# Batch norm with ReLU: the second half of x loaded as 14 and 2 rows per partition, its result stored in two transfers, and rows 4 to 15 of the first half in one

## The chip, the cores and the metric

One core of a Trainium2 chip. The metric is the device time of one execution in microseconds (us). Each ratio is to the kernel before in the same rounds; comparisons of traces cross chips.

## The reference

```python
# x: (32, 128, 32, 32) float32, 16.78 MB; the parameters: 128 values each
normalized = (x - running_mean[None, :, None, None]) / np.sqrt(running_var[None, :, None, None] + eps)
scaled = normalized * gamma[None, :, None, None] + beta[None, :, None, None]
return np.maximum(scaled, 0).astype(np.float32)
```

Each (image, channel) pair is a row of 1024 values, 4 KB. A row gets one scale and one bias, so ScalarE does it in one activation. The rest is moving 16.78 MB in and 16.78 MB out.

## The kernel before

x is seen as 2 halves of 128 partitions of 16 rows. A partition's 16 rows lie one after another in memory, 64 KB, so a transfer of n rows moves one run of 4n KB per partition. Loads are issued by SyncE, stores by ScalarE's queue.

```python
J = 16
TILES = ((0, 0, 2), (0, 2, 4), (0, 4, 8), (0, 8, 16), (1, 0, 16))   # half, first row, row after the last
LOAD_CUTS = {(1, 8)}      # a tile's load is cut here
STORE_CUTS = {(0, 1)}     # a store goes out before this row
HALVES = {(0, 0), (0, 1)} # rows done in two activations
...
    for t, a, b in TILES:
        xt = data.tile([P, b - a, HW], F32, name=f"x{t}_{a}")
        cuts = [a] + [j for j in range(a + 1, b) if (t, j) in LOAD_CUTS] + [b]
        for c, d in zip(cuts, cuts[1:]):
            nc.sync.dma_start(out=xt[:, c - a : d - a, :], in_=xr[t, :, c:d, :])
...
        for t, a, b, xt in tiles:                    # in this order on ScalarE
            first = a
            for j in range(a, b):
                # ... one ReLU activation (two for rows 0 and 1), in place
                if j + 1 == b or (t, j + 1) in STORE_CUTS:
                    nc.scalar.dma_start(
                        out=outr[t, :, first : j + 1, :], in_=xt[:, first - a : j + 1 - a, :]
                    )
                    first = j + 1
```

So before, the loads are 2, 2, 4, 8 rows of the first half and 8, 8 of the second; the stores are 1, 1, 2, 4, 8 rows of the first half and 16 of the second. The whole of x stays in on-chip memory; no buffer is used twice.

## Time and profile before

| | kernel before |
|---|---|
| median time, range of 3 runs | 83.81 us, 83.73 to 83.94 |
| span in the profile | 82.0 us |
| ScalarE busy | 39.1 us, 48% |
| first to last big DMA packet | 1.80 to 80.80 us, DMA busy share 1.00 |
| bytes | 16.78 MB read, 16.78 MB written |

The lines behind this are in the prediction. They are read like this: a busy share of 1.00 over all but 3 us means that the time is bytes over rate plus two ends; a wait of any other engine costs only if it leaves the DMA queues empty. One view belongs here too, because the change acts on it: the order of time of the second half on ScalarE (start, duration, engine, line, what, how often, and the wait ahead of it).

```profile
34.85 9.16 ACT L102 ACTIVATE x<-x,bias_t,scale_t 128x1024 f32<-128x1024 f32 x8 [1.78 <-DMA x<-in_x_dram]
46.87 9.16 ACT L102 ACTIVATE x<-x,bias_t,scale_t 128x1024 f32<-128x1024 f32 x8 [2.86 <-DMA x<-in_x_dram]
56.05 0.34 ACTq L110 DMA_DIRECT2D out_dram<-x  x1
```

Eight rows as soon as their load has landed, eight more after the next load, then one store of all sixteen.

### The profile page before, as it was taken

Reading aid. Unit: us, or ns where it says so; the run is one execution under the profiler, and the core shown is the slowest. Engines: PE = TensorE matmul, PEld = TensorE weight load, DVE = VectorE, ACT = ScalarE, POOL = GpSimd, SP = SyncE. Lnnn points to the kernel's source line nnn. Section 1 sums busy time; section 2 is a strip of 40 time slices with the busy share of each in tenths; the row PEclk is TensorE's granted clock in tenths of the full one; section 3 lists DMA queues with packets and bytes.
Section 4 is the critical chain, followed back from the end, with each engine's and each line's share of the span. In section 5 each row is a group of like instructions: output and inputs, shape, how many; then the busy total and the mean of one; then the engine's idle time right before and its main releaser. Section 6 shows DMA issues by size and latency. Waiting matters only on the chain.

```text
span 82.0 us, 120 instructions
## 1 busy us (share of the span) xinstructions
PE 0.7 (1%) x2; PEld 0.5 (1%) x2; DVE 0.8 (1%) x5; ACT 39.1 (48%) x36; POOL 0.8 (1%) x6
## 2 busy tenths in 40 slices
PE   0002000000000000000000000000000000000000
PEld 0002000000000000000000000000000000000000
DVE  0000300000000000000000000000000000000000
ACT  0600477799239999199994199993000000000000
POOL 3000000000000000000000000000000000000000
DMA  2899997979899989999799799998992999996590
GB/s 48 336 424 456 416 544 336 524 322 526 338 434 430 506 358 506 390 434 444 320 460 500 316 424 448 512 432 368 480 736 128 416 512 512 512 512 288 224 512 0
DMA packets 1792, 33.56 MB, mean 409 GB/s; under 512 B 256, under 2 KB 256, under 8 KB 512
## 3 DMA queue, kind: packets, MB, share of 16 engines
q1 hardware_dynamic: 864, 16.78, 48.7%
q10 hardware_dynamic: 928, 16.78, 47.6%
HBM read 16.78 MB, written 16.78 MB: 409 GB/s over the span
## 4 chain that ended last, share of the span: by engine, by line
DMA 56%; ACT 10%; issue 2%; SPq 0%
DMA x<-in_x_dram 56%; ACT x L102 10%; SPq L56 0%
## 5 line engine op out<-in xcount | busy, mean ns | idle before, releaser
L102 ACT ACTIVATE x<-x,bias_t,scale_t 128x1024 f32<-128x1024 f32 (+1 forms) x34 | 37.5, 1177 | 9.9 <-DMA x<-in_x_dram 7.6
L86 ACT ACT_TABLE_LOAD x1 | 1.3, 1283 | 2.6 <-issue 2.6
L86 ACT ACTIVATE std_t<-cols,eps_t 128x16 f32<-128x16 f32 x1 | 0.3, 273 | 4.5 <-PE cols L78 4.5
L78 PE MATMUL cols<-raw,rep 8*128 8x64 f32 x2 | 0.7, 429 | 7.6 <-DMA raw<-in_beta_dram 7.6
L78 PEld LDWEIGHTS cols<-raw,rep 8*128 8x128 f32 x2 | 0.5, 306 | 7.6 <-issue 7.6
L68 POOL TENSOR_SCALAR_AFFINE_SELECT rep<-rep 8x128 f32<-8x128 f32 x1 | 0.4, 392 | 0.1
L88 DVE RECIPROCAL rstd_t<-std_t 128x16 f32<-128x16 f32 x1 | 0.3, 254 | 7.7 <-ACT std_t L86 7.7
L67 POOL MEMSET rep<- 8x128 f32 x1 | 0.2, 194 | 0.3 <-POOLq L130 0.3
L90 DVE TENSOR_TENSOR scale_t<-cols,rstd_t 128x16 f32<-128x16 f32 x1 | 0.2, 175 | 0.1
L92 DVE TENSOR_TENSOR ms_t<-cols,scale_t 128x16 f32<-128x16 f32 x1 | 0.2, 175 | 0.0
L94 DVE TENSOR_TENSOR bias_t<-cols,ms_t 128x16 f32<-128x16 f32 x1 | 0.2, 174 | 0.0
L130 POOL MEMSET const-bfloat16-1.0<- 128x1 bf16 x1 | 0.1, 106 | 0.0
L130 POOL MEMSET const-uint8-127<- 128x1 uint8 x1 | 0.1, 106 | 0.0
L130 POOL MEMSET const-float32-0.0<- 128x1 f32 x1 | 0.1, 103 | 0.3 <-issue 0.3
L130 POOL MEMSET const-float32-1.0<- 128x1 f32 x1 | 0.1, 103 | 0.0
L65 DVE MEMSET eps_t<- 128x1 f32 x1 | 0.1, 59 | 0.9 <-PEq L130 0.9
## 6 DMA issues: line engine op xcount, KB each, us to landing
x<-in_x_dram SPq DMA_DIRECT2D x3, 4096.0 KB, 38.7
out_dram<-x ACTq DMA_DIRECT2D x1, 4096.0 KB, 28.7
x<-in_x_dram SPq DMA_DIRECT2D x2, 1024.0 KB, 5.8
x<-in_x_dram SPq DMA_DIRECT2D x1, 2048.0 KB, 11.3
out_dram<-x ACTq DMA_DIRECT2D x1, 2048.0 KB
out_dram<-x ACTq DMA_DIRECT2D x2, 512.0 KB, 19.6
out_dram<-x ACTq DMA_DIRECT2D x1, 1024.0 KB
raw<-in_running_var_dram ACTq DMA_DIRECT2D x1, 0.5 KB
```

What stands on the lines that cost most here:

```text
L65: nc.vector.memset(eps_t, float(eps))
L67: nc.gpsimd.memset(rep, 1.0)
L68: nc.gpsimd.affine_select(out=rep, in_=rep, compare_op=mybir.AluOpType.is_equal, fill=0.0, base=0, pattern=[[0, P // Q], [-1, Q]], channel ...
L78: nc.tensor.matmul(cols.rearrange("p k j -> p (k j)"), rep.rearrange("q r s -> q (r s)"), raw.rearrange("q k j -> q (k j)"), start=True, s ...
L86: nc.scalar.activation(out=std_t, in_=cols[:, 0, :], func=ACTF.Sqrt, bias=eps_t[:, 0:1], scale=1.0)
L88: nc.vector.reciprocal(out=rstd_t, in_=std_t)
L90: nc.vector.tensor_mul(out=scale_t, in0=cols[:, 1, :], in1=rstd_t)
L92: nc.vector.tensor_mul(out=ms_t, in0=cols[:, 2, :], in1=scale_t)
L94: nc.vector.tensor_sub(out=bias_t, in0=cols[:, 3, :], in1=ms_t)
L102: nc.scalar.activation(out=xt[:, j - a, w : w + step], in_=xt[:, j - a, w : w + step], func=ACTF.Relu, bias=bias_t[:, j : j + 1], scale=sc ...
L130: nc = _bacc.Bacc("TRN2", target_bir_lowering=False, num_devices=1)
```

## The change

Its apparent intent: give the load queue a long transfer and a short last one, and let half of the second half's result go out earlier, in place of one 8.39 MB store at the end.

```diff
-TILES = ((0, 0, 2), (0, 2, 4), (0, 4, 8), (0, 8, 16), (1, 0, 16))
+TILES = ((0, 0, 2), (0, 2, 4), (0, 4, 16), (1, 0, 16))
 
-LOAD_CUTS = {(1, 8)}
-STORE_CUTS = {(0, 1)}
+LOAD_CUTS = {(0, 8), (1, 14)}
+STORE_CUTS = {(0, 1), (1, 8)}
```

Loads after: 2, 2, 4, 8 and 14, 2. Stores after: 1, 1, 2, 12 and 8, 8.

## The prediction

> **What bounds the kernel now.** I read the page's slices first, then the DMA queues, then busy time by stage, and only then the chain of work that ended last. The kernel reads 16.78 MB and writes 16.78 MB, so the first question is whether the 16 DMA engines ever stand still. The page:
>
> ```profile
> span 82.0 us, 120 instructions
> PE 0.7 (1%) x2; PEld 0.5 (1%) x2; DVE 0.8 (1%) x5; ACT 39.1 (48%) x36; POOL 0.8 (1%) x6
> ...
> DMA  2899997979899989999799799998992999996590
> GB/s 48 336 424 456 416 544 336 524 322 526 338 434 430 506 358 506 390 434 444 320 460 500 316 424 448 512 432 368 480 736 128 416 512 512 512 512 288 224 512 0
> ...
> q1 hardware_dynamic: 864, 16.78, 48.7%
> q10 hardware_dynamic: 928, 16.78, 47.6%
> HBM read 16.78 MB, written 16.78 MB: 409 GB/s over the span
> ```
>
> ScalarE, the busiest compute engine, works 48% of the span. The two queues (q1 loads, q10 stores and the small parameters) take 48.7% + 47.6% = 96.3% of the 16 engines' time over the whole span. The DMA row seems to show holes (a 2 in the 31st slice, a 6 and a 5 near the end), with 736 GB/s just before one and 128 in it. I take these for an artefact: a slice is 2.05 us, and the packets of the last store, 64 KB each, take 2.418 us, so if a packet is booked where it starts, some slices get two rounds and some almost none. To check, I asked for longer stretches, cut where the trace's packet records change character: the first 8 KB packet starts at 1.80 us, the first store packet at 14.60, the last load packet ends at 46.17, the last store packet at 80.80.
>
> ```profile
> 1.80:14.60 12.80, 0.66 (x2) 0.50 (x2) 0.78 (x4) 5.64 (x7) 0.00 (x0) 1.00 1.03 420
> 14.60:46.20 31.60, 0.00 (x0) 0.00 (x0) 0.00 (x0) 24.26 (x22) 0.00 (x0) 1.00 1.00 422
> 46.20:80.80 34.60, 0.00 (x0) 0.00 (x0) 0.00 (x0) 9.16 (x8) 0.00 (x0) 1.00 0.99 429
> ...
> 0.00:1.80 1.80, 0.00 (x0) 0.00 (x0) 0.06 (x1) 0.00 (x0) 0.80 (x6) 1.00 0.00 0
> 1.80:80.80 79.00, 0.66 (x2) 0.50 (x2) 0.78 (x4) 39.06 (x36) 0.00 (x0) 1.00 1.00 425
> 80.80:82.00 1.20, 0.00 (x0) 0.00 (x0) 0.00 (x0) 0.00 (x0) 0.00 (x0) 1.00 0.00 0
> ```
>
> The second number from the end of each line is the DMA engines' busy share: 1.00 over 79.0 us. There are no holes. The span is 1.80 us before the first packet, 79.0 us of saturated DMA, 1.20 us after the last packet. The measured 83.81 us is about 1.8 us more than the span.
>
> Last, the chain, which would mislead if read first:
>
> ```profile
> 8.12 38.72 DMA x<-in_x_dram
> 46.84 0.03 issue
> 46.87 0.04 ACT x L102
> 46.91 1.10 issue
> 48.01 8.01 ACT x L102 x7
> ```
>
> It says: last load, eight activations, last store. But the last store, issued at 56.05 us, has its first packet only at 60.98: its queue was still busy with the store before it. The 8.39 MB of that store alone would be done by about 56.4 + 8.39/0.433 = 75.8 us; the end is 80.8. So the chain has some 4.9 us of slack here, and the bytes set the end.
>
> **What the Trainium skill says.** "DMA: Bandwidth & Descriptors", section Where 436 GB/s comes from, gives a ceiling of 435 GB/s for the 16 engines' ports. The trace agrees: 420 to 429 by stage as the lines count it, and 434 when I spread the packets of the store-only stage evenly over their durations. The same page, section Queues, rings and completion order, says that an engine takes turns between the queue rows that have work, a packet at a time. The trace agrees if one run of bytes per partition counts as the packet: between 14.60 and 35.67 us sixteen 4 KB store packets per engine went by, 1.32 us each, against 1.213 + 0.159 = 1.372 us for one 32 KB load packet plus one 4 KB store packet. "ScalarE: Activation LUTs", section What ACT_TABLE_LOAD costs, gives 186 ns + 0.833 ns per element plus about 93 ns for each per-partition operand: 186 + 853 + 186 = 1225 ns for 1024 elements with two. The trace has 1227 ns for the 30 rows of that shape.
>
> **The change, part by part.** Loads stay six, stores stay six; no byte is added; the activations stay 30 full rows and 4 half rows. The build of the changed kernel confirms it: the same instructions stand on PE, VectorE and GpSimd, and ScalarE and the load queue have other sizes only. The order of semaphore waits is alike too: activation rows still wait for their own load, not for the whole tile.
>
> *DMA work.* Packet times in the trace, by size: 4 KB 159 ns, 8 KB 309, 16 KB 611, 32 KB 1213, 64 KB 2418. That is a line: (2418 - 1213)/32768 = 0.0368 ns per byte plus about 8 ns per packet. From it, estimates for the new sizes: 56 KB 2117 ns, 48 KB 1816 ns. Each engine moves 8 partitions, so it has 8 packets per transfer, 96 in all, before and after. Before, per engine: loads 16 x 0.309 + 8 x 0.611 + 24 x 1.213, stores 16 x 0.159 + 8 x (0.309 + 0.611 + 1.213 + 2.418) = 38.94 + 38.95 = 77.9 us. The remaining 79.0 - 77.9 = 1.1 us is packets that took longer than these medians, about 0.95 us (0.47 at the start, 0.48 between 12 and 48 us, where reads and writes mix), and the engines' uneven start and end. After: loads 24 x 0.309 + 8 x (0.611 + 1.213 + 2.117) = 38.94, stores 16 x 0.159 + 8 x (0.309 + 1.816) + 16 x 1.213 = 38.95; sum 77.9 us. Change: 0.0 us.
>
> *Does any engine starve?* I walked one engine's queues by turns. Until the load of rows 8 to 15 lands nothing differs: ScalarE starts on them at 23.9 us, ends at 33.07, and the store of rows 4 to 15 is issued about 33.1, where the store of rows 8 to 15 was. By about 22.6 us six 4 KB store packets are through. Then eight turns of 56 KB load + 4 KB store: 8 x (2.117 + 0.159) = 18.2, to 40.8 us; the 14 rows land about 42 (in the before trace the landing of rows 8 to 15 came 1.2 us after the same reckoning). Then eight turns with the 8 KB loads, against two 4 KB and six 8 KB stores: 2 x 0.468 + 6 x 0.618 = 4.6, to 45.4 us, landing about 46.5. Loads thus end within 1 us of where they ended. At that point the store queue holds two 8 KB packets and eight 48 KB packets per engine: 0.6 + 14.5 = 15.1 us, enough until about 60.6.
>
> *ScalarE.* It starts the second half at about 42 instead of 34.85 us, 7 us later, but no longer pauses in the middle. Eight rows take 9.16 us, so the first store of the second half is issued about 51.2, needed at 60.6: 9 us in hand. The other eight end at about 60.4 (rows 14 and 15 are in by 46.5), the last store is issued then and needed at 60.6 + 8 x 1.213 = 70.3: 10 us in hand. Then 9.7 us more: 80.0, plus the engines' spread and the slow packets, 80.8 as before. So ScalarE ending some 4 us later than its 56.0 costs nothing, and splitting the last store gains nothing.
>
> Sum: 1.8 + 79.0 + 1.2 = 82.0 us of span, 83.8 us measured.
>
> **The rivals.**
> 1. *The last store is the tail, and halving it shortens the end.* For it: the chain. Against it: DMA share 0.99 to 1.00 to the end. If the chain did bind, ScalarE's end at 60.4 plus 4.19 MB at 0.433 would give about 70 us for the last packet, so 73 us measured. I see no way for 33.5 MB to move in that time.
> 2. *The later ScalarE starves the stores.* It would need the 48 KB store or the first store of the second half to come more than 9 us later than worked out, for instance if its activations waited for the whole tile and the second half's first store went out at 55 to 56 us: still before 60.6. If both second-half stores were held until the very end, ScalarE's 60.4 plus about 3 us of issue to first packet, the hole would be about 3 us: 86.8 us.
> 3. *The mix of reads and writes moves at another rate.* The mixed stage lost 0.48 us to slow packets. Larger load packets leave fewer changes between read and write per megabyte before 41 us and more of them after. That can give back or cost up to that amount: 83.3 to 84.3.
> 4. *A 56 KB or 48 KB run is not moved as one packet.* 64 KB runs are one packet each in the trace, so I expect it. If the 56 KB loads were cut into 4 KB packets, 1664 more packets at 8 ns over 16 engines would be 0.8 us, and taking turns would favour the stores: 84.6 us.
>
> **Range and chances.** Everything that I can size comes to zero within rival 3; the three runs before span 83.73 to 83.94. I predict 83.8 us, 83.3 to 84.3 in 8 of 10 cases. Faster by 2% needs 82.1 us, below what 79 us of saturated DMA plus the two ends and the 1.8 us outside the span allow even without a single slow packet (83.81 - 0.95 = 82.9): 0.01. Slower by 2% is 85.5, which only a starved stage gives (rival 2): 0.02. Within 2%: 0.97.
>
> **What would show it right or wrong.** In the profile of the changed kernel: DMA share near 1.00 from about 1.8 to 80.8 us; 96 packets per engine again, with 128 packets of 56 KB at about 2.12 us and 128 of 48 KB at about 1.82; ScalarE's second half from about 42 to 60.4 us with one wait before it; the last load landing about 46.5; the last store issued about 60.4 and its first packet near 70. It would be wrong if a stretch after 46 us showed a DMA share clearly under 1, if the new sizes appeared as many small packets, or if the packet times of known sizes grew.

## The result, and the profile after

| | before | after |
|---|---|---|
| median of 6 runs each | 83.77 us | 84.18 us |
| range | 83.6 to 83.94 | 84.01 to 84.31 |
| span of the profiled run | 82.0 us | 82.4 us |
| first to last big packet | 1.80 to 80.80 us | 1.81 to 81.19 us |

The ratio is 1.0047, with a 95% interval of 1.0030 to 1.0064. Executions over 1.5% slower than the fastest of the same kernel are left out of the means. Ratios here are the mean time of one kernel's fast runs over that of the other's of the same rounds, so not quite the ratio of the medians. The prediction (83.8 us, 83.3 to 84.3, within 2%) holds; the change is some 0.4 us slower, which is small but clear of the noise. The span belongs to one profiled run; before, that run took 83.68 us and not the median 83.81, so the time lies 1.7 us above the span in both kernels, not the 1.8 of the prediction.

From the page of the changed kernel:

```profile
span 82.4 us, 120 instructions
...
DMA  2899997979799999999489988888996998899690
GB/s 48 318 434 466 414 533 334 549 302 557 302 509 454 469 477 477 477 450 336 169 330 430 712 382 382 382 382 382 573 430 302 477 509 382 382 509 461 302 509 0
...
q1 hardware_dynamic: 864, 16.78, 48.9%
q10 hardware_dynamic: 928, 16.78, 47.4%
```

The packet counts, 864 and 928, are those of before: 96 data packets per engine, as counted in the prediction. The queues' shares sum to 96.3%, again as before. By stage, cut at the first and last big packet (after the name of the stretch its length, the busy time of PE, its weight loads, VectorE, ScalarE and GpSimd, the clock, the DMA share and GB/s):

```profile
0.00:1.81 1.81, 0.00 (x0) 0.00 (x0) 0.06 (x1) 0.00 (x0) 0.79 (x6) 1.00 0.00 0
1.81:81.19 79.38, 0.66 (x2) 0.50 (x2) 0.77 (x4) 39.06 (x36) 0.00 (x0) 1.00 1.00 423
81.19:82.40 1.21, 0.00 (x0) 0.00 (x0) 0.00 (x0) 0.00 (x0) 0.00 (x0) 1.00 0.00 0
```

The two ends are unchanged (1.81 and 1.21 us). The saturated part is 79.38 us instead of 79.00, still at a share of 1.00: the engines do not wait more, they take longer for the same packets. And ScalarE in order of time:

```profile
42.52 9.16 ACT L102 ACTIVATE x<-x,bias_t,scale_t 128x1024 f32<-128x1024 f32 x8 [9.49 <-DMA x<-in_x_dram]
51.70 0.34 ACTq L110 DMA_DIRECT2D out_dram<-x  x1
52.09 9.16 ACT L102 ACTIVATE x<-x,bias_t,scale_t 128x1024 f32<-128x1024 f32 x8 [0.42 <-ACT x L102]
61.27 0.34 ACTq L110 DMA_DIRECT2D out_dram<-x  x1
```

ScalarE waits 9.49 us for the 14 rows, starts the second half 7.7 us later than before and issues the last store 5.2 us later. None of this reaches the end: the first store of the second half goes out at 51.70 us, and the store ahead of it keeps its queue busy until 61.4 to 61.8.

Where are the 0.4 us? In the packet records of the traces, the time of one 56 KB load packet has a median of 2116 ns (the estimate was 2117), but a mean of 2182. All the excess is in one round: each of the 16 engines moves eight such packets, and the last one, begun between 38.7 and 39.4 us, took 2641 ns on average, 25% longer. The other seven of each engine took 2116. (The records carry no engine number; the starts fall into eight bands of 16, and each band is taken for one round.) ScalarE stood idle from 33.4 to 42.52 us, so it is not what slowed that round. From here on I call "slow-packet time" what an engine's load packets begun between 26 and 48 us take beyond the usual time of their size (the medians of before and 912, 1815 and 2116 ns for 24, 48 and 56 KB), averaged over the 16 engines: 0.19 us before, 0.64 us after.

### The profile page after: what moved, and what is told of

It reads as the page before. It is cut to its first block, busy times and chain, and to the rows that moved or that the text cites. A ratio compares the mean times of both kernels' runs of the same rounds, so it can differ in the third digit from the quotient of the medians.

```text
span 82.4 us, 120 instructions
## 1 busy us (share of the span) xinstructions
PE 0.7 (1%) x2; PEld 0.5 (1%) x2; DVE 0.8 (1%) x5; ACT 39.1 (47%) x36; POOL 0.8 (1%) x6
## 4 chain that ended last, share of the span: by engine, by line
DMA 49%; ACT 21%; ACTq 1%; issue 1%
DMA x<-in_x_dram 43%; ACT x L102 21%; DMA raw<-in_running_mean_dram 6%; ACTq L63 1%; ACTq L110 0%
## 5 line engine op out<-in xcount | busy, mean ns | idle before, releaser
L102 ACT ACTIVATE x<-x,bias_t,scale_t 128x1024 f32<-128x1024 f32 (+1 forms) x34 | 37.5, 1177 | 15.2 <-DMA x<-in_x_dram 12.5
```

The source lines that it names most:

```text
L102: nc.scalar.activation(out=xt[:, j - a, w : w + step], in_=xt[:, j - a, w : w + step], func=ACTF.Relu, bias=bias_t[:, j : j + 1], scale=sc ...
```

## The experiments

Two theories to start with. A: the 0.4 us comes with the load cut, as slow load packets. B: it comes from the stores. Beside them the old claim had to be tested that ScalarE's lateness costs nothing as long as the store queue is full, against the chain of waits, which says the opposite.

### 1. The load cut alone

```diff
-LOAD_CUTS = {(1, 8)}
+LOAD_CUTS = {(1, 14)}
```

> Only the load cut moves: second half read as 14 and 2 rows, stores as in the kernel before. Theory A (the extra 0.4 us of the changed kernel is its slow last round of 56 KB load packets): about +0.4 us, ratio 1.003 to 1.006, and 56 KB packets with a mean near 2.18 us, the slow ones all in the last of an engine's eight. Rival B (the stores cost it: the 48 KB store, or the last store in two): 0.0, ratio 0.998 to 1.002, 56 KB packets near 2.12 us.

Measured: 84.28 us, ratio 1.0056 (1.0038 to 1.0073). 56 KB packets have a mean of 2202 ns; the slow ones, 2807 ns on average, are again each engine's last of eight. Slow-packet time 0.83 us. This is theory A. (Runs 1 and 2 were made in the same rounds, and their intervals do not touch.) ScalarE, in order of time:

```profile
42.68 18.20 ACT L102 ACTIVATE x<-x,bias_t,scale_t 128x1024 f32<-128x1024 f32 x16 [9.63 <-DMA x<-in_x_dram]
60.91 0.34 ACTq L110 DMA_DIRECT2D out_dram<-x  x1
```

With one store for the whole half it is issued at 60.91 us. Its first packet begins at 61.76, and the store ahead of it ends on the engines between then and 62.17: by the packet records the engines stand idle 0.03 us on average. The load cut alone uses up the whole slack of before, and no more.

### 2. The store cut alone

```diff
-TILES = ((0, 0, 2), (0, 2, 4), (0, 4, 8), (0, 8, 16), (1, 0, 16))
+TILES = ((0, 0, 2), (0, 2, 4), (0, 4, 16), (1, 0, 16))
-LOAD_CUTS = {(1, 8)}
-STORE_CUTS = {(0, 1)}
+LOAD_CUTS = {(0, 8), (1, 8)}
+STORE_CUTS = {(0, 1), (1, 8)}
```

> Only the stores move: rows 4 to 15 as one transfer, second half as two, loads 8 and 8 rows as before. Theory A: 0.0, ratio 0.998 to 1.002. Rival B: about +0.4 us, ratio 1.003 to 1.006. If neither this run nor the load cut alone shows it, it needs both together.

Measured: 83.82 us, ratio 0.9994 (0.9972 to 1.0015); slow-packet time 0.41 us. Splitting the last store and joining the earlier ones is worth nothing by itself, as the prediction had it, and B falls.

### 3 and 4. One load of 16 rows; 2 rows and then 14

```diff
-LOAD_CUTS = {(1, 8)}
+LOAD_CUTS = set()
```

```diff
-LOAD_CUTS = {(1, 8)}
+LOAD_CUTS = {(1, 2)}
```

> The second half read as one load of 16 rows, 64 KB packets, stores as before. If the last packet of a long load is slow in proportion to its size whatever follows it (A1): the last 64 KB load packet of each engine takes 0.5 us or more over the 2.42 us of the others, time +0.2 to +0.5 us. If it is the 8 KB loads behind a long packet that slow it (A2): no slow last packet, time within 0.1 us of before.

> The second half read as 2 and then 14 rows, stores as before: the 56 KB packets are there, but nothing is queued behind them. A1 (last packet of a long load): slow last 56 KB packets again, mean near 2.18 us, time +0.3 to +0.5 us. A2 (the 8 KB loads behind them): 56 KB packets near 2.12 us, time within 0.15 us of before.

Measured: 86.98 us, ratio 1.0377, and 86.48 us, ratio 1.0310. Neither expectation had this: I had looked at the load packets only, although the slack of the last store could be worked out. The one load, in order of time on ScalarE, and two stretches of the same trace (columns as above):

```profile
45.22 18.20 ACT L102 ACTIVATE x<-x,bias_t,scale_t 128x1024 f32<-128x1024 f32 x16 [12.43 <-DMA x<-in_x_dram]
63.45 0.34 ACTq L110 DMA_DIRECT2D out_dram<-x  x1
...
48.00:61.00 13.00, 0.00 (x0) 0.00 (x0) 0.00 (x0) 13.00 (x12) 0.00 (x0) 1.00 1.03 445
62.20:64.20 2.00, 0.00 (x0) 0.00 (x0) 0.00 (x0) 1.22 (x2) 0.00 (x0) 1.00 0.00 0
```

The store is issued at 63.45 us, and its first packet begins at 64.29; the store queue has been empty since 61.5 to 62.1. Here the DMA engines do stand still, 2.61 us on average by the packet records, and 2.65 us in the other kernel (store issued at 63.12). A warning on the reading: a stretch of 2 us with a share of 0.00 is no proof, because packets are booked where they begin and a 64 KB packet takes 2.4 us. The same stretch shows 0.00 in the load cut alone, where nothing stood still. The packet records and the 3 us in the time settle it.

As to the slow packets: in the one load the last 64 KB packet of each engine took 3282 ns on average against 2418 for the others (slow-packet time 0.87 us). In "2 then 14" the last 56 KB packets took 2175, hardly slow (0.06 us), but the last two rounds of the load ahead, of 32 KB packets between 20 and 22 us, were slow instead (0.43 us). So "the last packet of a long load is slow" is not the whole rule, and neither A1 nor A2 fits both runs.

### 5 and 6. ScalarE delayed on purpose

In the changed kernel, after the first row of the second half, n useless activations on a zeroed scratch tile (its setting up is cut here), n = 6 and n = 12:

```diff
+                if (t, j) == (1, 0):
+                    for _ in range(n):
+                        nc.scalar.activation(out=junk, in_=junk, func=ACTF.Relu,
+                                             bias=bias_t[:, 0:1], scale=scale_t[:, 0:1])
```

> The changed kernel, with six useless 128x1024 activations after the first row of the second half (6 x 1.145 = 6.9 us of ScalarE time). Slack theory: the first store of the second half goes out near 58.6 instead of 51.7 us and its queue is busy until 61.4, the last near 68.2 and its queue is busy until 71.1: no hole, time as the changed kernel, 84.0 to 84.4 us. Rival (the chain from load over ScalarE to the last store sets the end): +6.9 us, about 91 us.

> The same with twelve useless activations (13.7 us). Slack theory: the first store of the second half goes out near 65.4, first packet 0.85 us later (as in the run with one load: 63.45 to 64.29), queue empty since 61.4 to 61.8: a hole of about 4.6 us, none before the last store (75.0 + 0.85 against 76.0), time about 88.8 us (88.2 to 89.4). Chain theory: +13.7 us, about 97.9 us.

Measured: six take 7.6 us of ScalarE's time and the kernel 84.37 us, ratio 1.0080 (1.0060 to 1.0100) to before, against 1.0047 (1.0030 to 1.0064) of the changed kernel in other rounds: the difference is 0.3 us of 7.6, and the intervals meet. No engine idles between 50 and 80 us. Twelve take 15.2 us and the kernel 90.77 us:

```profile
43.50 15.23 ACT L114 ACTIVATE junk<-junk,bias_t,scale_t 128x1024 f32<-128x1024 f32 x12
58.63 8.01 ACT L105 ACTIVATE x<-x,bias_t,scale_t 128x1024 f32<-128x1024 f32 x7
66.67 0.34 ACTq L122 DMA_DIRECT2D out_dram<-x  x1
...
62.20:67.40 5.20, 0.00 (x0) 0.00 (x0) 0.00 (x0) 4.78 (x5) 0.00 (x0) 1.00 0.00 0
67.40:86.00 18.60, 0.00 (x0) 0.00 (x0) 0.00 (x0) 8.82 (x8) 0.00 (x0) 1.00 1.05 450
```

The store goes out at 66.67 us, its first packet begins at 67.52, and the engines idle 5.89 us on average: 84.18 + 5.9 = 90.1, near the 90.77. My 88.8 was too low because I took 1.145 us for a useless activation, the spacing of the real ones, which each work on a row of their own; these, all on one tile, took 1.27. That the one tile is the reason is not shown. The chain theory's 91 and 97.9 us are far off. The slack theory is shown: with six, the first store of the second half went out 7.5 us later (59.20 us) and no engine idled; with twelve, 15.0 us later, and of that the 6.2 us beyond the slack of 8.8 (see below) came back as 5.9 us of idle engines.

### 7. One load, with the stores of the changed kernel

```diff
 (the changed kernel)
-LOAD_CUTS = {(0, 8), (1, 14)}
+LOAD_CUTS = {(0, 8)}
```

> The second half read as one load of 16 rows, with the stores of the changed kernel (rows 4 to 15 as one, second half in two). If the 3.2 us of the one load with one last store came from that store's late issue (63.45 us, its queue empty since 61.5 to 62.1), the hole goes: first store of the second half near 54.4, last near 63.5. What stays is the slow last 64 KB load round: 84.2 to 84.7 us, ratio 1.004 to 1.010 to before. If the hole had another cause, about 87 us.

Measured: 84.50 us, ratio 1.0097 (1.0079 to 1.0116). The first store of the second half goes out at 54.62 us, the engines no longer idle, and 2.5 of the 3.2 us are back. What is left, 0.8 us by the ratio, goes with the largest slow-packet time of all, 1.03 us. So the store cut is not without use: it is what makes a long load affordable.

### 8. No store beside the loads

In the changed kernel, ScalarE takes the second half first and waits for its last row before it begins, so that all stores come after all loads.

```diff
+    last = params.tile([P, 1], F32, name="last")
-        for t, a, b, xt in tiles:
+        for t, a, b, xt in tiles[::-1]:
             first = a
+            if t == 1:
+                nc.scalar.copy(out=last, in_=xt[:, b - 1, 0:1])
```

> The changed kernel's loads, but ScalarE first waits for rows 14 and 15 of the second half and takes that half first, so that no store packet runs beside a load (time some 92 us, of no interest). If the last long load round is slow because of the stores beside it: all 56 KB packets at about 2.12 us. If it is slow by itself, ahead of short loads or the end of the loads: the last 56 KB packet of each engine 0.4 to 0.7 us longer again, mean near 2.18 us.

Measured: one run, 98.94 us (more than the 92 guessed; the stores wait for ScalarE twice). 56 KB packets have a mean of 2129 ns. The last round took 2140 ns on average and the seven before it 2127, so there is no slow last round here; all eight rounds together lie 0.10 us per engine above 2116. This is what the expectation had for stores as a condition of the slow round. It is one trace, and the run also takes ScalarE's work away from the time of the loads.

### 9 and 10. Loads of 8, 6, 2 and of 12, 4 rows

```diff
 (the changed kernel)
-LOAD_CUTS = {(0, 8), (1, 14)}
+LOAD_CUTS = {(0, 8), (1, 8), (1, 14)}
```

```diff
 (the changed kernel)
-LOAD_CUTS = {(0, 8), (1, 14)}
+LOAD_CUTS = {(0, 8), (1, 12)}
```

> The changed kernel with its 14-row load cut into 8 and 6 rows (loads 8, 6, 2; one transfer more, 8 packets more per engine at 8 ns, 0.06 us). If the cost of the change is the size of the last long load packet: the last 24 KB load packets lose at most 0.15 us, time 83.7 to 84.0 us, ratio 0.999 to 1.003. If the cost is the 8 KB loads at the end, which are still there: ratio 1.004 to 1.006.

> The changed kernel with loads of 12 and 4 rows. Size theory: the last 48 KB packet of each engine 0.3 to 0.45 us longer than the others, between the 32 KB packets (0.1 to 0.3) and the 56 KB ones (0.45 to 0.65); time ratio 1.002 to 1.005. If only the 8 KB loads behind matter: no slow last 48 KB packets, ratio within 0.002 of 1.

Measured: 84.47 us, ratio 1.0104 (1.0087 to 1.0121), above both branches of its expectation, and 83.99 us, ratio 1.0048 (1.0032 to 1.0064). The theory that the size of the last long packet sets the loss falls with the first: its 24 KB packets were slow in many rounds, with a mean of 1002 ns against 912 at best (slow-packet time 0.82 us). Its short loads also took turns with 48 KB store packets and ended only at 58.6 us; nothing starved, though. In the second, the last 48 KB packets were slow by only 0.15 us, not 0.3 to 0.45, and 16 KB packets behind them were slow too. Its slow-packet time of 0.48 us is close to that of 8 and 8, though its ratio says 0.4 us. The comparison crosses chips: its span, 82.15 us, is 0.2 us above that of the trace before, while the kernel before took only 83.52 us in its rounds, and has no trace there.

### 11. Rows 0 and 1 as one store

```diff
 (the changed kernel)
-LOAD_CUTS = {(0, 8), (1, 14)}
-STORE_CUTS = {(0, 1), (1, 8)}
+LOAD_CUTS = {(0, 8), (1, 8)}
+STORE_CUTS = {(1, 8)}
```

> An attempt to beat both: loads 8 and 8, stores of the changed kernel, but rows 0 and 1 as one store (8 packets fewer per engine, 0.06 us). If 4 KB stores beside the loads are what slows some load rounds, the slow rounds shrink and up to 0.4 us goes: ratio 0.995 to 0.999. If not: 0.998 to 1.001, that is, no difference that can be told.

Measured: 84.42 us, ratio 1.0098 (1.0083 to 1.0114): 0.8 us slower, outside both branches. The attempt failed. Its last loads took turns with 48 KB store packets and ended only at 54.4 us, but no engine idled. The trace shows a slow-packet time of 0.06 us late, but 0.54 us between 10 and 26 us, and the measured time lies 2.1 us above the span in place of 1.7. I did not follow that up, so this loss with loads of 8 and 8 is unexplained. No kernel of this study beats the one before.

### 12. The kernel before against itself

> The kernel before, unchanged, against itself, to see how much of a ratio and of the slow load packets is chance. Time ratio 0.998 to 1.002. If the extra slow packets between 36 and 48 us belong to the 14-row load, this trace has 0.2 to 0.4 us per engine of them there, as the two traces with loads of 8 and 8 rows (0.19 and 0.41), and not 0.6 to 0.85 as the four with 14 and 2 (0.64, 0.83, 0.79, 0.77).

Measured: 83.87 us, ratio 1.0017 (0.9991 to 1.0044). The slow-packet time is 0.47 us, above the 0.2 to 0.4 that I had written and below 0.6. The interval of this control reaches 1.0044; the 1.0047 of the changed kernel and the 1.0056 of run 1 lie above it with little to spare.

The slow-packet times, from the packet records, one trace each:

| loads of the second half | us per engine, 26 to 48 us |
|---|---|
| 8, 8 with two stores of single rows (before, store cut alone, before again) | 0.19, 0.41, 0.47 |
| 14, 2 (after, load cut alone, delay 6, delay 12) | 0.64, 0.83, 0.79, 0.77 |
| 16 (one load, one load with two stores) | 0.87, 1.03 |
| 12, 4 | 0.48 |
| 8, 6, 2 | 0.82 |
| 2, 14 | 0.06 (0.64 between 10 and 26 us) |
| 8, 8 with rows 0 and 1 as one store | 0.06 (0.54 between 10 and 26 us) |

The means of the first two lines are 0.36 and 0.76: a difference of 0.40 us, the size of what the change cost.

Counted over all loads instead of 26 to 48 us, the same sum goes with the span in all ten traces in which no engine idled: 0.95 us at a span of 81.97 (before), 1.05 to 1.19 at 82.15 to 82.25 (store cut alone, before again, 12 and 4, rows 0 and 1 as one store), 1.29 at 82.36 (after), 1.44 to 1.55 at 82.45 to 82.92 (delay 6, load cut alone, one load with two stores, loads of 8, 6 and 2). Slow load packets thus carry most of the differences in span, wherever in the loads they fall. The two traces of the kernel before differ by 0.2 us in both.

## Why the prediction was right, and by what it missed

- **The bound.** Right, and shown: a DMA share of 1.00 from 1.81 to 81.19 us, and no idle engine after 50 us. The experiments with delays show the claim behind it: lateness of ScalarE is free until the store queue runs empty. The slack of the kernel before was 4.1 us and not the 4.9 worked out, because a store also needs 0.85 us from issue to first packet.
- **The same packets.** Right: 96 per engine; 56 KB at a median of 2.116 us (2.117 estimated), 48 KB at 1.815 (1.816). Its sign of being wrong, that known sizes take longer, did not show in the medians: what grew was the mean of a new size.
- **The walk by turns.** Right within a microsecond: the second half starts on ScalarE at 42.52 us (42 said), its stores go out at 51.70 and 61.27 (51.2 and 60.4), the last load packet ends at 46.70 (46.5), the store of 12 rows at 61.4 to 61.8 (60.6), the last store begins near 71.1 (70.3).
- **The slack of some 9 us.** Right in kind, a little generous: 51.70 + 0.85 for the first packet leaves 8.8 us until 61.4.
- **"The sum is 0.0 us."** Here the miss lies: the term for packets that take longer than their median, 0.95 us, was carried over unchanged, with up to half a microsecond either way left to rival 3. In the trace it is 1.29 us: the last round of 56 KB loads alone takes 0.53, the rest 0.76. The load cut brings it, not the stores (runs 1 and 2). Rival 3 had named the place, the mixed stage, and a bound; it had not said which way. That the time stayed under 84.3 is in part luck: nothing had shown that the slow packets could not grow by more than they had been (run 1, with the same loads of 14 and 2, took 84.28 us).
- **Rival 2** named the right danger for the wrong kernel. In the change as it stands no store starves. Run 1 is close to its worst case, all of the second half held until ScalarE's end, and lost nothing there: the first packet came 0.85 us after the issue and not 3, so there was no hole of 3 us (84.28 us and not 86.8). But that used up the room that the last store had: its issue came 4.9 us later than before, the end of the queue ahead of it only 0.8 us, and a slightly longer load (run 3) or a later one (run 4) starves it by 2.6 us. The store cut gives that room back. The prediction weighed the sum only, and said that the split gains nothing; by itself that is so.

What stays open is why those load packets are slow. That they need stores beside them is suggested by run 8, in one trace; their size does not decide it (run 9), nor that short loads follow (run 3 has none). I have no theory that fits all traces.

## What to carry to other kernels

When the DMA engines are busy from end to end, count packets and bytes before and after, and then only ask whether any queue runs empty: the answer is the issue time of each transfer against the time at which the queue ahead of it ends. A rearrangement that is free at the end may still spend such slack; the one load of 16 rows cost 3.2 us with one last store (run 3) and 0.8 us with a split one (run 7), though the split alone was worth nothing (run 2). Below half a per cent, the time of single packets matters, and it is to be measured, not carried over.

## What the Trainium skill lacked or had wrong

- "DMA: Bandwidth & Descriptors", section SWDGE vs HWDGE vs iDMA, calls a packet, the boundary at which an engine changes between queues, "≤4096 B preferably, ≤64 descriptors", in a table on what GpSimd builds. For these loads and stores, issued from SyncE and ScalarE, a run of up to 64 KB went through as one record of 2418 ns, and the two queues took turns run by run. The page lacks the consequence: while 32 KB loads ran against 4 KB stores (1.32 us a turn) in the kernel before, stores got 25 to 70 of some 430 GB/s in stretches of 2 us, 50 on average.
- No page tabulates the time of one run by its size for transfers issued from SyncE and ScalarE. Here: 4 KB 159 ns, 8 KB 309, 16 KB 611, 32 KB 1213, 48 KB 1815, 56 KB 2116, 64 KB 2418; that is 0.0368 ns per byte and about 8 ns per run.
- "DMA: Bandwidth & Descriptors", section Latency and other measured facts, gives some 600 ns to the first byte for transfers issued from SyncE and ScalarE. The page doesn't say from when it counts. With its queue empty and the engines idle, the first packet of a store began 0.84 to 0.85 us after its issue began (63.45 to 64.29, 63.12 to 63.96, 66.67 to 67.52), which is 0.5 us after the 0.34 us of issuing. Beside running loads it was far more, although the store queue was empty too: the first store of the kernel before was issued at 11.16 us and its first packet began at 14.60, and the other runs with stores beside loads took 3.4 to 4.5 us.
- No page speaks of load packets that slow down late in the loads: 2641 instead of 2116 ns for the last 56 KB packet of each engine, up to 3451 instead of 2418 for 64 KB (run 7), with an engine's other seven at the usual time.
